# An attention unit's loads taken forward, transposes ahead of products, and a last row reordered, in a fused decoder block

## The chip, the cores and the metric

The kernel runs on one core of one Trainium2 chip. The metric is the device time of one execution in microseconds; lower is better. The version before takes 911.03 us, the median of 3 runs (910.79 to 912.06). The execution that was profiled took 911.87 us, and its span from the first to the last instruction is 910.2 us.

The core has four computing engines, each with its own queue of instructions that it takes strictly in order: TensorE (PE in the profile, its weight loads PEld), VectorE (DVE), ScalarE (ACT) and GpSimd (POOL). SyncE (SP) only issues transfers. Transfers issued by SP, POOL or ACT run on the same 16 DMA engines.

## The reference

One block of a decoder for 1024 tokens of width 1024, in float32:

```
h     = rmsnorm(x, norm_g) * (1 + scale) + shift      # scale, shift, gate from c @ w_ada
q, k, v, g_attn, xr, g_rnn, m_attn, m_rnn = split(h @ w_in)
q, k  = partial rotary embedding                       # 16 heads of 64, 4 of k and v
y_attn = window_attention(q, k, v, sinks) * silu(g_attn)     # window of 128 tokens
xr    = causal convolution of width 4
y_rnn = rg_lru(xr) * silu(g_rnn)                       # a scan along the tokens
merged = sigmoid(m_attn) * (y_attn @ w_attn_proj) + sigmoid(m_rnn) * (y_rnn @ w_rnn_proj)
x     = x + gate * (merged @ w_out)
out   = rmsnorm(x, final_g)
```

The attention works in blocks of 128 tokens: each block of queries sees its own block of keys and the one before, under a band mask, and a learned sink per head stands in the denominator.

## The kernel before

Every float32 operand of a large product is split into a rounded high part and the rest, and each product is made of three (high x high, high x low, low x high). Large products are tiled 128 x 128 against 512 columns and use one step of Strassen's scheme, so that a pair of output chunks takes seven slots of twelve matmuls each (`product`, line 709). Splitting the weights is the helper pair of lines 105 (ScalarE casts the high part, `wh`) and 111 (VectorE subtracts, `wl`).

The stages follow each other on TensorE: the start (to some 90 us), the seven-slot products of the projections with the gates of the recurrent branch between them (to some 557 us), attention in 32 units, between which the last projection slots and then the recurrent output projection (`rp`) are laid (to some 735 us), the projection of attention, and the output projection with the final norm in the tail (to the end). From the start to the end of attention the order on every engine is the order in which the program is written (a manual schedule); there is no scheduler in between. The functions that put work into slots keep estimated costs, but the change does not touch those.

The recurrent branch, per 128 channels: `conv(ic)` makes the convolved input `xc` on ScalarE (`base`, line 902) and VectorE (`tap`), in tiles that hold 4 KB per partition, two of them. Gate products follow, and `after_gates` computes the recurrence; its step `d2` (line 1053) multiplies by `xc` for the last time. In the last group of channels (c = KC - 1 = 7) that is the last use of any `xc` tile.

Attention. `open_attn` opens the memory pools of this stage and issues the first loads (two pairs of keys and queries, and the values). `load_kq(m)` loads the keys (`ks`) and queries (`qs`) of two units; there are two buffers. A unit u of the loop runs, on the engines named:

- `scores`: eight matmuls into `s_ps` (PE, line 1324); PSUM holds one `s_ps`, so the next scores need the last VectorE reading of this one
- `maxima_a`, `maxima_d`: copy to `p` (ACT, 1333), mask (DVE, 1339; in the first unit of a group POOL, 1342) and row maximum (DVE, 1344)
- `weights_a(u-1)`: four exponentials (ACT, 1349)
- pieces of the projections (one slot of twelve matmuls on PE, with their casts and subtractions)
- `weights_d(u-1)`: division by the denominator (DVE, 1355 and 1356)
- `values(u-3)`: up to four products with `v` into `pv` (PE, 1397), of `phc`, `plc` and their masked copies `phm`, `plm`
- `join_a`, `join_d` (u-3): two copies `ob` of 64 partitions (ACT, 1406 and 1407) and two adds into `yq` (DVE, 1417 and 1418)
- `transposed(u-2)`: four transposes of `p` into `pt` (PE, 1363)
- `split_a`, `split_d` (u-2): `phc` (ACT, 1368) and `plc` (DVE, 1374) from `pt`
- `masks(u-2)`: `phm` and `plm` (POOL, 1383)

`phc`, `plc`, `phm`, `plm`, `pt` and `pv` have one buffer each.

The tail. Each of eight rows of 128 tokens gets its output products, an add of the residual (`add_to`, DVE, line 1867), a sum of squares (`square`, ACT, 1871), a root (`root`, ACT, 1882), a reciprocal (DVE, 1886), a scaling of one half on DVE (1887) and of the other on ACT (1889), and one store. The second half of each row enters last. For rows 4 to 7 that is the left half (LEFT), and the right half has been multiplied by the final weight before. Row 7 is made in two parts of 256 columns, c1 and c2, and stored in two halves by SP and ACT. The tail too is in written order on PE, ACT and DVE.

## Time and profile before

| what | us |
|---|---|
| median of 3 runs | 911.03 |
| the profiled execution | 911.87 |
| its span | 910.2 |
| PE busy | 896.9 |
| DVE busy | 718.4 |
| ACT busy | 566.6 |
| POOL busy | 128.7 |

A row of a timeline reads: start and duration in us, engine, line of the kernel, operation, output <- inputs, shapes, how many were merged, and in brackets how long the engine had stood idle before it and what ended that. A row of the stretches reads: from and to, length, busy time and count for PE, PEld, DVE, ACT and POOL, then the clock that TensorE was granted (1.00 is full), the busy share of the DMA engines and their GB/s. A row of the chain of waits has start, duration and what ran. Ends of matmuls are modelled and overlap the next one's start, so the starts are what counts.

### The profile page before, as it was taken

The page shows a single profiled execution, that of the slowest core. Times are in us where ns is not written, and L with a number is a line of the kernel's source. Part 1 is how long each engine was busy: PE and PEld are TensorE (multiplying, and loading weights), DVE is VectorE, ACT ScalarE, POOL GpSimd, SP SyncE. Part 2 cuts the span into 40 slices and gives each one's busy share as a digit, 9 for nine tenths or more (in the row PEclk, how much of TensorE's full clock was granted, in tenths as well). Part 3 has the DMA queues.
Part 4 walks back from the last instruction along what each step waited for, and adds up shares of the span by engine and source line. Part 5 has one row for each costly group of instructions (what it writes and reads, how often), then busy time and mean ns, then how long its engine had stood idle before and what let it go on. Part 6 is the DMA issues. An engine that isn't in the chain of part 4 may idle for free.

```text
span 910.2 us, 12600 instructions
## 1 busy us (share of the span) xinstructions
PE 896.9 (99%) x4258; PEld 746.8 (82%) x4259; DVE 718.4 (79%) x1071; ACT 566.6 (62%) x1102; POOL 128.7 (14%) x216
## 2 busy tenths in 40 slices
PE   9999999999999999999999998999999999999996
PEld 6789888888888888888888887888888888888885
DVE  6997688988669875897797796899999847668855
ACT  7965554654566855777585874888888632115435
POOL 7420241200000000000000002353443400000000
PEclk9999999999999999999999999999999999999999
DMA  9828589862435353354535367996656289416604
GB/s 361 329 78 276 168 264 321 254 219 93 150 131 194 128 209 137 125 196 142 169 140 177 107 205 251 322 396 213 220 201 213 73 302 368 139 47 231 208 1 184
DMA packets 87203, 180.71 MB, mean 199 GB/s; under 512 B 8626, under 2 KB 29122, under 8 KB 87140
## 3 DMA queue, kind: packets, MB, share of 16 engines
q1 hardware_dynamic: 83056, 167.07, 52.3%
q0 software_dynamic: 3936, 12.59, 4.3%
q8 instruction: 33, 0.54, 0.2%
q14 instruction: 30, 0.25, 0.1%
q10 hardware_dynamic: 148, 0.27, 0.1%
HBM read 121.34 MB, written 58.95 MB: 198 GB/s over the span
## 4 chain that ended last, share of the span: by engine, by line
PE 91%; DVE 5%; ACT 2%; issue 1%; DMA 1%; POOL 0%; SPq 0%; DVEq 0%; ACTq 0%
PE bk L709 47%; PE rp L173 13%; PE out L1853 6%; PE pmain L173 5%; PE pgate L1022 5%; PE s_ps L1324 3%; PE pv L1397 2%; PE pmain L485 2%; PE bk L485 2%; PE pt L1363 1%; PE pmain L1574 1%; PE pmain L1573 1%; PE pmain L1572 1%; DMA qs<-q_d 1%; ACT jk L1871 1%
## 5 line engine op out<-in xcount | busy, mean ns | idle before, releaser
L709 PE MATMUL bk<-nl,wh 128*128 128x512 f32 x368 | 143.9, 391 | 0.0
L709 PE MATMUL bk<-nh,wh 128*128 128x512 f32 x368 | 143.8, 391 | 0.0
L709 PE MATMUL bk<-nh,wl 128*128 128x512 f32 x368 | 99.0, 391 | 0.0
L111 DVE TENSOR_TENSOR wl<-r,wh 128x512 fp32r<-128x512 f32 x109 | 79.2, 733 | 22.2 <-ACT wh L105 22.2
L105 ACT CAST wh<-r 128x512 fp32r<-128x512 f32 x107 | 65.5, 618 | 29.1 <-PE rp L173 9.8
L709 PEld LDWEIGHTS bk<-nh,wl 128*128 128x128 f32 x368 | 69.6, 189 | 14.6
L709 PEld LDWEIGHTS bk<-nh,wh 128*128 128x128 f32 x368 | 69.4, 189 | 14.5
L709 PEld LDWEIGHTS bk<-nl,wh 128*128 128x128 f32 x368 | 69.3, 188 | 14.3
L709 PE MATMUL bk<-hl,wh 128*128 128x512 f32 x184 | 71.6, 389 | 0.0
L709 PE MATMUL bk<-hh,wh 128*128 128x512 f32 x184 | 71.6, 389 | 0.0
L111 DVE TENSOR_TENSOR wl<-ws,wh 128x512 fp32r<-128x512 f32 x76 | 52.0, 685 | 7.1 <-ACT wh L105 7.0
L62 POOL DMA_DIRECT2D yh_d<-av x1 | 0.6, 569 | 371.6 <-ACT av L1085 371.6
L1349 ACT ACTIVATE p<-p,small 128x129 f32<-128x129 f32 x128 | 50.1, 401 | 0.0
L709 PE MATMUL bk<-hh,wl 128*128 128x512 f32 x184 | 49.2, 389 | 0.0
L105 ACT CAST wh<-ws 128x512 fp32r<-128x512 f32 x76 | 46.0, 614 | 4.7 <-DVE ws L731 2.3
L709 PEld LDWEIGHTS bk<-hh,wl 128*128 128x128 f32 x184 | 34.5, 188 | 7.2
L709 PEld LDWEIGHTS bk<-hh,wh 128*128 128x128 f32 x184 | 34.6, 188 | 7.1
L709 PEld LDWEIGHTS bk<-hl,wh 128*128 128x128 f32 x184 | 34.5, 188 | 7.1
L1324 PE MATMUL s_ps<-ks,qs 128*128 128x256 f32 (+1 forms) x256 | 37.6, 289 | 2.7 <-DMA qs<-q_d 2.5
L709 PE MATMUL bk<-hha,wh 128*128 128x512 f32 x92 | 35.8, 389 | 0.0
L709 PE MATMUL bk<-hla,wh 128*128 128x512 f32 x92 | 35.8, 389 | 0.0
L1324 PEld LDWEIGHTS s_ps<-ks,qs 128*128 128x128 f32 x256 | 32.4, 189 | 3.7 <-issue 2.8
(375 smaller groups left out, 2294.1 us busy)
## 6 DMA issues: line engine op xcount, KB each, us to landing
r<-w_main SPq DMA_DIRECT2D x100, 256.0 KB, 4.3
wada<-w_ss SPq DMA_DIRECT2D x16, 512.0 KB, 9.0
qs<-q_d SPq DMA_DIRECT2D x16, 512.0 KB, 5.1
wo_d<-wr SPq DMA_DIRECT2D x28, 256.0 KB, 2.9
wo<-wo_d SPq DMA_DIRECT2D x14, 512.0 KB, 5.3
ks<-k_d SPq DMA_DIRECT2D x12, 384.0 KB, 4.0
xt<-x SPq DMA_DIRECT2D x8, 512.0 KB, 6.6
sma_d<-c SPq DMA_DIRECT2D x16, 256.0 KB, 4.5
```

The source lines that it names most:

```text
L105: A.copy(dst[0][:], src)
L111: V.tensor_tensor(out=dst[1][:], in0=src, in1=f32(dst[0][:]), op=ALU.subtract)
L173: mm = T.matmul(ps[hf], ww, xx[kc][hf], start=(kc == 0 and ww is w_h and xx is xh), stop=(kc == KC - 1 and xx is xl))
L485: T.matmul(starts[c][hf], ww[:, c0:c0 + P], xh[kc][hf], start=(kc == 0 and t_ == "h"), stop=(kc == KC - 1 and t_ == "l"))
L709: W["pe"] = T.matmul(ps, ww[:, kc * P:(kc + 1) * P], b[kc][i], start=(first and n == 0), stop=(n == 11), skip_group_check=not first)
L1022: W["pe"] = T.matmul(ps[:, SL[hf]], ww[:, c0:c0 + P], xx_[:, SL[hf]], start=(ic == 0 and i == 0), stop=(ic == 1 and i == 2))
L1324: W["pe"] = T.matmul(o, qs[:, j, qc], ks[:, kb:n % 2 + 2, b, :], start=(b == 0), stop=(b == 1))
L1349: A.activation(px[:, j, :], px[:, j, :], AF.Exp, bias=sm[:, 0, j:j + 1], accum_out=sm[:, 1, j:j + 1])
L1363: W["pe"] = T.transpose(pt[:, j, :], px[:, j, 0:P], ident[:])
L1397: W["pe"] = T.matmul(pv[:], b, m[:].rearrange("p j q -> p (j q)"), start=(i == 0), stop=(i == len(prods) - 1))
L1572: T.matmul(o, hh[kc][th][:, ts_], wh[:, cols], start=(kc == 0), stop=False)
L1853: T.matmul(o, a[k][x_][:, p * P:(p + 1) * P], b[k][y_][:, cols], start=(first and k == 0 and i == 0), stop=(k == 3 and i == 2), skip_group ...
```

## The change

Three edits that do not depend on each other.

First, the tiles `xc` of the convolution get a pool of their own, at the other end of the memory (the right side, where the tiles of v's preparation stood before). As soon as the last multiplication by `xc` is written, that pool is closed, a pool for the keys and queries of even pairs of units takes its place, and the first load of keys and queries is issued there and then. `open_attn` opens only the pool for odd pairs and loads the second pair. Second, within a unit the transposes go ahead of the products with v, and the splits ahead of the joins. Third, the tail: row 7's squares are summed on DVE instead of ACT, and row 7's second add and square go ahead of the scaling of row 6's left half and of row 6's store; row 7's left half is scaled by root and weight in one instruction instead of two products with the weight and one with the root.

```diff
--- before.py
+++ after.py
@@ -872,8 +872,11 @@
 
     rn_ctx = ExitStack()
 
+    xc_ctx = ExitStack()
+
     def open_rnn():
         rope_ctx.close()
+        W["xcp"] = pool(xc_ctx, "xcp", bufs=2, side="right")
         W["rn"] = pool(rn_ctx, "rnn")
 
     def xr_sinks(hb):
@@ -898,7 +901,7 @@
                 x_ = xr[ic]
 
                 def base():
-                    t["xc"] = W["rn"].tile([P, S], F32, tag="xc", name="xc", bufs=2)
+                    t["xc"] = W["xcp"].tile([P, S], F32, tag="xc", name="xc")
                     A.activation(t["xc"][:], x_[:], AF.Identity,
                                  scale=pcol(PK_CW + 24, c), bias=pcol(PK_CB, c))
 
@@ -1052,6 +1055,10 @@
         def d2():
             V.tensor_tensor(out=t["it"][:], in0=t["it"][:], in1=W["xc", hb, oc][2][:],
                             op=ALU.mult)
+            if c == KC - 1:
+                xc_ctx.close()
+                W["kq", 0] = pool(at_ctx, "kq0", side="right")
+                load_kq(0)
 
         def a3():
             A.activation(tl("th"), t["rz"][:], AF.Tanh)
@@ -1276,23 +1283,22 @@
         nonlocal at, psx
         psm_ctx.close()
         psx = pool(psx_ctx, "psx", space=PSUM)
-        W["kq"] = pool(at_ctx, "kq", bufs=2, side="right")
+        W["kq", 1] = pool(at_ctx, "kq1", side="right")
         W["yo"] = pool(at_ctx, "yo", side="right")
         W["pp"] = pool(at_ctx, "pp", bufs=3, side="right")
         W["pp"].tile([P, 72], F32, name="pad", bufs=1)
         at = pool(at_ctx, "at", side="right")
-        load_kq(0)
+        load_kq(1)
         load_v(0)
-        load_kq(1)
 
     def load_kq(m):
         g, t0 = m // 4, (m % 4) * 256
-        ks = W["kq"].tile([P, 3, 2, P], F32R, tag="ks", name="ks")
+        ks = W["kq", m % 2].tile([P, 3, 2, P], F32R, tag="ks", name="ks")
         kv = k_d.rearrange("(p j) n b t -> j p n b t", j=4)[g]
         n0 = t0 // P
         lo = 1 if t0 == 0 else 0
         dma(ks[:, lo:, :, :], kv[:, n0 - 1 + lo:n0 + 2, :, :])
-        qs = W["kq"].tile([P, 4, 256], F32R, tag="qs", name="qs")
+        qs = W["kq", m % 2].tile([P, 4, 256], F32R, tag="qs", name="qs")
         dma(qs[:], q_d[g][m % 4].rearrange("(a j) t -> a j t", j=4))
         U["kq", m] = ks, qs
 
@@ -1701,14 +1707,16 @@
         flush()
         if 1 <= u < 33:
             weights_d(u - 1)
+        if 2 <= u < 34:
+            transposed(u - 2)
         if u >= 3:
             values(u - 3)
+        if 2 <= u < 34:
+            split_a(u - 2)
+            split_d(u - 2)
+        if u >= 3:
             join_a(u - 3)
             join_d(u - 3)
-        if 2 <= u < 34:
-            transposed(u - 2)
-            split_a(u - 2)
-            split_d(u - 2)
         if u + 1 < 32:
             sink(u + 1)
         while own_stores:
@@ -1941,23 +1949,32 @@
             result(4 + p, RIGHT, LEFT)
     c1, c2 = slice(0, 256), cut
     f = fs[:, 7, :]
+
+    def square_d(sl, acc):
+        jk = tail.tile([P, 2, HALF], F32, tag="S", name="xg", bufs=4)[:, 0, 0:256]
+        V.scalar_tensor_tensor(out=jk, in0=xo[7][:, sl], scalar=1.0, in1=xo[7][:, sl],
+                               op0=ALU.mult, op1=ALU.mult, accum_out=acc)
+
     gemm(pa[3][:, c1], A22, wt4, 3, cols=c1)
     add_to(7, c1, pa[3][:, c1])
-    square(7, c1, f[:, 1:2])
-    result(6, RIGHT, LEFT)
-    xg = tail.tile([P, 2, HALF], F32, tag="S", name="xg", bufs=4)[:, 0, :]
-    V.tensor_tensor(out=xg[:, c1], in0=xo[7][:, c1], in1=fg_bc[:, c1], op=ALU.mult)
+    square_d(c1, f[:, 1:2])
     V.scalar_tensor_tensor(out=f[:, 0:1], in0=f[:, 1:2], scalar=1.0 / D, in1=f[:, 0:1],
                            op0=ALU.mult, op1=ALU.add)
+    r6 = fs[:, 6, 3:4]
+    V.reciprocal(r6, fs[:, 6, 2:3])
+    A.activation(xo[6][:, RIGHT], xo[6][:, RIGHT], AF.Copy, scale=r6)
     gemm(end, A22, wt4, 3, cols=c2)
     add_to(7, c2, end)
-    square(7, c2, f[:, 1:2])
+    square_d(c2, f[:, 1:2])
+    V.scalar_tensor_tensor(out=xo[6][:, LEFT], in0=xo[6][:, LEFT], scalar=r6,
+                           in1=fg_bc[:, LEFT], op0=ALU.mult, op1=ALU.mult)
+    dma(out[6 * P:7 * P, :], xo[6][:])
     root(7)
-    V.tensor_tensor(out=xg[:, c2], in0=xo[7][:, c2], in1=fg_bc[:, c2], op=ALU.mult)
     V.reciprocal(f[:, 3:4], f[:, 2:3])
     A.activation(xo[7][:, RIGHT], xo[7][:, RIGHT], AF.Copy, scale=f[:, 3:4])
-    V.tensor_scalar(out=xg, in0=xg, scalar1=f[:, 3:4], scalar2=None, op0=ALU.mult)
-    dma(out[7 * P:, LEFT], xg)
+    V.scalar_tensor_tensor(out=xo[7][:, LEFT], in0=xo[7][:, LEFT], scalar=f[:, 3:4],
+                           in1=fg_bc[:, LEFT], op0=ALU.mult, op1=ALU.mult)
+    dma(out[7 * P:, LEFT], xo[7][:, LEFT])
     dma(out[7 * P:, RIGHT], xo[7][:, RIGHT], A)
     last.close()
 
```

SP's issues around the first edit, as one piece of the difference; `r` are weights of the projections, `gg` a gate, `wo_d` and `ga_d` stores of intermediate results:

```order
 L62 DMA gg<-sgr_d_135 128x1024
 L62 DMA r<-w_main 128x512
+L62 DMA ks<-k_d 128x512
+L62 DMA qs<-q_d_89 128x1024
 L62 DMA wo_d_140<-wr 128x512
 L62 DMA ga_d_94<-c 128x2x256
```

The same two loads stood behind two stores of `wo_d`, directly ahead of the second pair of ks and qs; now these fourteen rows of the old order, sixteen transfers, lie behind them, and the second pair follows after them.

TensorE in a unit of attention, before; then the same place with the change (its line numbers are 6 higher):

```order
L173 MATMUL rp_5727<-yl,wh 128x512 x2
L1397 MATMUL pv<-phc,vd 128x512
L1397 MATMUL pv<-plc,vd 128x512
L1397 MATMUL pv<-phm,vd 128x512
L1397 MATMUL pv<-plm,vd 128x512
L1363 MATMUL pt<-ident,p 128x128 x4
L1324 MATMUL s_ps<-ks,qs 128x256 x8
```

With the change:

```order
L173 MATMUL rp_5734<-yl,wh 128x512 x2
L1369 MATMUL pt<-ident,p 128x128 x4
L1403 MATMUL pv<-phc,vd 128x512
L1403 MATMUL pv<-plc,vd 128x512
L1403 MATMUL pv<-phm,vd 128x512
L1403 MATMUL pv<-plm,vd 128x512
L1330 MATMUL s_ps<-ks,qs 128x256 x8
```

The transposes moved past the four products; the scores stay last. On ScalarE and VectorE the split of the weights moved past the joins in the same way.

VectorE at the end, before; `xo` is a row, `rbig` holds the sums and roots, `xg` the weighted left half of row 7 (below: scratch for the squares):

```order
L1867 TENSOR_TENSOR xo<-xo,out_8241 128x256
L1886 RECIPROCAL rbig<-rbig 128x1
L1887 SCALAR_TENSOR_TENSOR xo<-xo,rbig,fg_bc 128x512
L1949 TENSOR_TENSOR xg<-xo,fg_bc 128x256
L1950 SCALAR_TENSOR_TENSOR rbig<-rbig 128x1
L1867 TENSOR_TENSOR xo<-xo,out_8242 128x256
L1956 TENSOR_TENSOR xg<-xo,fg_bc 128x256
L1957 RECIPROCAL rbig<-rbig 128x1
L1959 TENSOR_SCALAR xg<-xg,rbig 128x512
```

With the change:

```order
L1875 TENSOR_TENSOR xo<-xo,out_8249 128x256
L1955 SCALAR_TENSOR_TENSOR xg,rbig<-xo 128x256
L1961 SCALAR_TENSOR_TENSOR rbig<-rbig 128x1
L1964 RECIPROCAL rbig<-rbig 128x1
L1875 TENSOR_TENSOR xo<-xo,out_8250 128x256
L1955 SCALAR_TENSOR_TENSOR xg,rbig<-xo 128x256
L1969 SCALAR_TENSOR_TENSOR xo<-xo,rbig,fg_bc 128x512
L1973 RECIPROCAL rbig<-rbig 128x1
L1975 SCALAR_TENSOR_TENSOR xo<-xo,rbig,fg_bc 128x512
```

The scaling of row 6 (1887 before, 1969 now) stood ahead of row 7's second add and now stands behind it and its square.

## The prediction

> **What bounds the kernel now.** I read the page first, then the chain of waits in order of time, then the stretches on that chain that are not TensorE's, each by its timeline.
>
> ```profile
> PE 896.9 (99%) x4258; PEld 746.8 (82%) x4259; DVE 718.4 (79%) x1071; ACT 566.6 (62%) x1102; POOL 128.7 (14%) x216
> PE 91%; DVE 5%; ACT 2%; issue 1%; DMA 1%; POOL 0%; SPq 0%; DVEq 0%; ACTq 0%
> ```
>
> TensorE sets the time, so an edit pays only where TensorE stands still, runs slowly, or has finished. The chain leaves it in three places after the start-up: near 557, between 583 and 609, and from 884 on.
>
> First place, the entry to attention. The rows are the timelines of TensorE, VectorE and SP, a row of the chain, and three stretches with the granted clock behind the five busy times:
>
> ```profile
> 556.52 1.07 PE L709 MATMUL bk<-nh,wl 128*128 128x512 f32 x4
> 552.63 7.28 DMA qs<-q_d
> 560.04 1.08 PE L1324 MATMUL s_ps<-ks,qs 128*128 128x128 f32 x8 [2.45 <-DMA qs<-q_d]
> 557.43:560.04 2.61, 0.16 (x2) 0.03 (x1) 0.00 (x0) 0.00 (x0) 0.00 (x0) 1.00 1.02 385
> 560.04:565.36 5.32, 5.32 (x21) 4.36 (x22) 2.49 (x4) 1.59 (x3) 0.92 (x3) 0.68 0.99 358
> 565.36:569.05 3.69, 3.69 (x21) 3.21 (x20) 1.82 (x3) 2.54 (x11) 0.00 (x0) 1.00 0.65 207
> ...
> 522.39 0.42 SPq L62 DMA_DIRECT2D r<-w_main  x1
> 525.27 1.20 DVE L1053 TENSOR_TENSOR it<-it,xc 128x1024 f32<-128x1024 f32 x1
> 527.70 0.38 SPq L62 DMA_DIRECT2D ga_d<-c  x1
> 538.64 0.95 SPq L62 DMA_DIRECT2D r<-w_main  x2
> 545.75 5.33 SPq L62 DMA_DIRECT2D ga_d<-c  x2
> 554.96 0.36 SPq L62 DMA_DIRECT2D qs<-q_d  x1
> ```
>
> The first scores wait for qs, which takes 7.28 us because the DMA engines are full (share 1.02) and because its issue stood behind a store that held SP for 5.33 us. Matmuls of 512 columns start 0.23 us apart (two of them make the 0.46 between two kinds of unit, below), so after the four of 556.52 the scores could have started at 557.43. The wait costs 2.61 us. There is a second cost: after it the same work, eight score matmuls and twelve of 512 columns, takes 5.32 us at a clock of 0.68, and 3.69 at 1.00. The short form of unit 0 is worth some 0.03, so 5.32 - 3.66 = 1.66 us are lost to the clock.
>
> Second place, the units of attention. One starts with each s_ps:
>
> ```profile
> 587.78 1.19 PE L1324 MATMUL s_ps<-ks,qs 128*128 128x256 f32 x8
> 592.82 1.19 PE L1324 MATMUL s_ps<-ks,qs 128*128 128x256 f32 x8
> 597.48 0.51 PE L1397 MATMUL pv<-plm,vd 128*128 128x512 f32 x1
> 598.18 1.09 PE L1324 MATMUL s_ps<-ks,qs 128*128 128x128 f32 x8
> 603.16 1.19 PE L1324 MATMUL s_ps<-ks,qs 128*128 128x256 f32 x8
> 608.71 1.22 PE L1324 MATMUL s_ps<-ks,qs 128*128 128x256 f32 x8 [0.24 <-DVE p L1339]
> 614.06 1.19 PE L1324 MATMUL s_ps<-ks,qs 128*128 128x256 f32 x8
> 618.64 1.19 PE L1324 MATMUL s_ps<-ks,qs 128*128 128x256 f32 x8
> 623.88 1.22 PE L1324 MATMUL s_ps<-ks,qs 128*128 128x256 f32 x8
> ```
>
> A unit without a stall takes 592.82 - 587.78 = 5.04 us. The others show 5.36, 5.55, 5.35 and 5.24: 0.32 + 0.51 + 0.31 + 0.20 = 1.34 us lost in all. (The unit from 614.06 has two products with v less, hence 4.58.) Two of the stalls, 0.32 and 0.31, stand before the fourth product (plm, the mask that POOL makes last); two before the scores, which need VectorE's p. I count on nothing from the later units.
>
> Third place, the tail.
>
> ```profile
> 902.50 0.30 ACT L1882 ACTIVATE rbig<-rbig 128x1 f32<-128x1 f32 x1
> 903.03 0.75 DVE L1887 SCALAR_TENSOR_TENSOR xo<-xo,rbig,fg_bc 128x512 f32<-128x512 f32 x1
> 903.85 0.33 SPq L62 DMA_DIRECT2D out<-xo  x1
> 904.11 0.41 DVE L1867 TENSOR_TENSOR xo<-xo,out 128x256 f32<-128x256 f32 x1
> 904.61 0.42 ACT L1871 ACTIVATE jk<-xo 128x256 bf16<-128x256 f32 x1 [0.80 <-DVE xo L1867]
> 905.68 0.72 ACT L1958 ACTIVATE xo<-xo,rbig 128x512 f32<-128x512 f32 x1 [0.23 <-DVE rbig L1957]
> 906.20 0.33 SPq L62 DMA_DIRECT2D out<-xg  x1
> 906.43 0.38 ACTq L62 DMA_DIRECT2D out<-xo  x1
> 902.56 0.28 PE L1853 MATMUL out<-wo,ml 128*128 128x256 f32 x1
> GB/s 0 0 0 0 0 0 0 0 0 0 0 322 354 0 148 412 116 0 386 291 0 206 412 58 32 391 254 0 248 412 16 79 407 190 37 391 248 0 0 0
> ```
>
> TensorE ends at 902.84, but the last add waits until 904.11 behind row 6's scaling; the last issue is at 906.43 and the span ends at 910.2. The rates are in steps of 0.775 us from 880: row 6 moves from about 904.65 to 905.94 (0.80 us after its issue), row 7 from about 907.05 to 908.39, both at about 400 GB/s.
>
> **The change part by part.** *The early load.* ks and qs of unit 0 move from behind the store of 545.75 to behind the r of 522.39, and SP then waits for the product with xc, 525.27 + 1.20 = 526.47. Two issues of some 0.4 each (the rows of SP) end at about 527.3; with even the old 7.28 us they land by 535, 22 us before use. Behind them on SP stand a store of wo_d, the ga_d of 527.70 and two stores of y. None is loaded soon, and the next loads that weights need are those of 538.64, which today wait for another store. I cost the move at nothing; SP would have to be held some 11 us more before those loads suffer. The convolution tiles change their place, and the first one now waits for stores of v's parts instead of stores of q, which are older: nothing. Next late in the same place would be the second pair of loads, issued by 554.96; with even 9 us they are there at 564, and unit 2 would need them at 569.05 - 4.27 = 564.78. That is the thinnest cover, and 0.79 MB less in front of it makes it thicker. So 2.61 us go. With no gap I expect the clock to stay at 1.00, and 1.66 more go: **-4.27**. From below: only the wait, -2.6; from above -4.4.
>
> [...] The row speaks for the gap, as 0.68 stands right behind it.
>
> *The order within a unit.* No instruction is added or removed. The four transposes (5.04 less 3.69 for scores and twelve products, less 0.91, so 0.44 us) pass ahead of the four products with v (4 x 0.23 = 0.91), and the splits ahead of the joins on ScalarE and VectorE. So pt ends 0.91 us earlier, phc no longer waits for two copies on ScalarE, plc no longer stands behind two joins on VectorE, and the products are wanted 0.44 later. VectorE falls behind here for two reasons, the first row and the fourth:
>
> ```profile
> 589.06 0.42 DVE L1417 TENSOR_TENSOR yq<-pv,ob 64x256 f32<-64x256 f32 x1 [0.61 <-ACT ob L1407]
> 596.25 0.68 DVE L1532 TENSOR_TENSOR yq<-yq,r 128x512 f32<-128x512 f32 x1
> 600.79 1.11 POOL L1383 TENSOR_SCALAR_AFFINE_SELECT plm<-plc 128x512 fp32r<-128x512 f32 x1 [0.65 <-DVE plc L1374]
> 601.32 1.12 DVE L1532 TENSOR_TENSOR yq<-yq,r 128x512 f32<-128x512 f32 x1
> ...
> 594.74 0.59 ACT L1368 CAST phc<-pt 128x512 fp32r<-128x512 f32 x1
> ```
>
> It waits 0.61 us for the copies (a wait that remains, since plc now waits for phc instead), and the same instruction takes 1.12 beside POOL's mask and 0.68 alone. After the change the two joins stand right behind plc, so they run beside that mask, and they read PSUM. Standing behind plc, the joins let plm start 2 x 0.42 us sooner, which covers the stalls of 0.32 and 0.31; each overlap that falls away gives VectorE 0.44 back before the scores at 608.71 and 623.88. The most is 1.34. The least is nothing: if VectorE keeps its pace, TensorE only arrives earlier and waits for p instead (rival A). A loss would need a longer loop through the single phc buffer (rival E). I take **-1.2**, near the upper end, as plm's lead is the larger effect.
>
> [...]
>
> *The tail.* Two squares leave ScalarE for VectorE, two products with the final weight vanish into one scaling, and row 6's scaling of the left half and its store pass behind row 7's last add. Nearest rows for the square with its sum:
>
> ```profile
> 18.60 1.26 DVE L275 SCALAR_TENSOR_TENSOR jk<-wada,c_bc 128x1024 bf16<-128x1024 f32 x1
> 19.79 0.08 DVE L275 DVE_READ_ACCUMULATOR jk<-wada,c_bc 128x1 f32 x1
> ```
>
> For 256 columns it lies between an add of that width (0.41) and a scaling of 512 (0.75); by the slope 0.75 to 1.26 I take 0.49, and 0.08 for the sum. The first square falls into VectorE's wait for the root of row 6, which ends at 902.80. The reciprocal ends near 903.0, as now; the add follows at once (now at 904.11), the square from 903.43 to 904.0, row 6's scaling to 904.75: its store is issued at 904.77, 0.92 later than now. The root of row 7 runs beside that; its reciprocal ends near 904.91, the last scalings near 905.66, and the last issue is at 905.68 against 906.43, 0.75 earlier. But now two rows follow each other: row 6 would start at 904.77 + 0.80 = 905.57, and 2 x 0.524 MB at 400 GB/s take 2.62, so 908.19 against 908.39. **-0.2**; -0.75 if the transfers pack better, +0.3 if the square with its sum costs 0.3 more each and row 6 goes out later still.
>
> Sum: -4.27 - 1.2 - 0.2 = -5.7. The profiled execution took 911.87 us around a span of 910.2; the span becomes 904.5 and that time 906.2. The median of the runs shown, 911.03, lies 0.84 below the profiled one; I take the difference from it: **905.3 us**.
>
> **The rivals.**
>
> A. VectorE keeps setting the pace of attention. For: its wait of 0.61 stays in another place, and it was late by itself at 608.71. Against: the 0.44 of each overlap that goes is its own time. Only the entry and the tail pay: 911.03 - 4.47 = 906.6.
>
> B. The slow clock stays although the gap has gone: -2.61 - 1.2 - 0.2, so 907.0. Against it: 1.00 both before and after the one slow stretch.
>
> C. The DMA engines become the wait. The rows show shares of 1.02 and 0.99, and TensorE now comes 4.3 us sooner to operands of y that pass through the same engines. For relief there are 0.79 MB less (128 x 1536 words; 2.0 us at 400 GB/s) and the free third of 565 to 569 (0.35 x 3.69 = 1.3 us): 4.27 - 2.0 - 1.3 = 1.0 us could be given back, 906.3; with unit 2's keys late as well, up to 907.4. Against: today no product waits for a transfer but the first.
>
> D. The early load does not end the wait, because something else holds the first scores. Then -1.4, 909.6, which is no change. Against: all other needs of that instruction are met long before.
>
> E. Slower. phc has one buffer. Its next writer must now wait for a product that stands behind the transposes, so a loop closes: transposes 0.44, product 0.23, phc 0.59, plc at most 0.75 (a scaling of that width), plm 1.11, with some 0.4 for hand-overs 3.5 us. It decides when it passes the period of 5.04. If ScalarE's other work put 1.8 us into it, each further 0.25 over 29 units would cost 7.2: 911.03 - 4.5 + 7.2 = 913.7. Against: 1.5 us of room.
>
> **How the numbers follow.** Forecast 0.57 (its own range 904.3 to 906.2), A 0.14, B 0.07, C 0.10, D 0.05, E 0.04, and 0.03 for more than the forecast (all three upper ends give -4.4 - 1.34 - 0.75, 904.5, and stalls that I did not count). A measurement of this kernel tells 0.2% (1.8 us) from no change, so A, B and C count as faster: 0.91, same 0.05, slower 0.04. The range for 8 in 10 leaves out D, E and the ends: 904.2 to 907.5.
>
> **What would show it.** Right: TensorE without a gap at 557, a clock of 1.00 from 557 to 566, and 3.66 us from the first scores to the second; periods of 5.04 up to 624; the last issue some 0.8 us nearer to TensorE's end, with DMA rates at 400 GB/s unbroken over the last two rows. Wrong: a gap at 557 with another releaser (D); a slow clock with no gap (B); s_ps that waits for p with periods above 5.2 (A); a product that waits for yh, yl or ks (C); periods above 5.04 in all units with phc as releaser (E). The prediction fails as a whole if TensorE's end in the tail does not move by over 4 us.

## The result

The changed kernel takes 907.68 us, the median of 6 runs (907.29 to 908.05), beside 911.45 for the kernel before (6 runs, 909.81 to 912.79). The ratio is 0.9959 with a 95% interval of 0.9946 to 0.9972: 0.4% faster. A second comparison on another chip gave 907.62 beside 911.75 and a ratio of 0.9953 (0.9936 to 0.9970). The direction was forecast; 905.3 was too low by 2.4 us, and 907.68 lies just outside the range. The profiled execution took 907.33 us, with a span of 905.5.

The page of the changed kernel, in the order of the two rows that the prediction began with, and one group:

```profile
PE 894.3 (99%) x4259; PEld 746.1 (82%) x4259; DVE 718.6 (79%) x1073; ACT 567.2 (63%) x1098; POOL 121.1 (13%) x216
PE 93%; DVE 4%; ACT 2%; issue 1%; DVEq 0%; ACTq 0%
L111 DVE TENSOR_TENSOR wl<-r,wh 128x512 fp32r<-128x512 f32 x109 | 75.0, 695 | 24.0 <-ACT wh L105 23.7
```

The transfer of qs has left the chain of waits, and TensorE's share of it rose from 91% to 93%. POOL's busy time fell from 128.7 to 121.1 us without an instruction less: the 28 masks plm take 632 ns in the mean, against 979 before.

The first place, the entry to attention, in the timeline of TensorE and as three stretches (from and to, length, busy time of the five engines, granted clock, share of the DMA engines, GB/s):

```profile
556.85 1.07 PE L709 MATMUL bk<-nh,wl 128*128 128x512 f32 x4
557.75 1.00 PE L1330 MATMUL s_ps<-ks,qs 128*128 128x128 f32 x8
552.00:557.75 5.75, 5.75 (x27) 4.74 (x26) 4.56 (x7) 1.62 (x3) 3.35 (x4) 1.00 1.00 304
557.75:561.43 3.68, 3.68 (x22) 3.15 (x21) 0.00 (x0) 1.59 (x3) 0.64 (x1) 1.00 0.98 367
561.43:565.13 3.70, 3.70 (x22) 3.21 (x21) 3.38 (x6) 2.55 (x11) 0.31 (x2) 1.00 0.71 264
```

The scores start 0.90 us after the start of the last group of four matmuls, without a gap. The clock is 1.00 throughout, and unit 0 takes 3.68 us, although the DMA engines are still full (0.98).

The second place, the units. Rows of TensorE, then of VectorE and POOL in the same stretch:

```profile
599.15 1.11 PE L1330 MATMUL s_ps<-ks,qs 128*128 128x256 f32 x8
605.00 1.22 PE L1330 MATMUL s_ps<-ks,qs 128*128 128x256 f32 x8 [0.63 <-DVE p L1345]
597.27 1.10 DVE L1548 TENSOR_TENSOR al<-yq,ah 128x512 fp32r<-128x512 f32 x1
...
600.30 1.06 DVE L1362 TENSOR_TENSOR p<-p,small 128x512 f32<-128x512 f32 x1
...
602.42 0.43 DVE L1424 TENSOR_TENSOR yq<-pv,ob 64x256 f32<-64x256 f32 x1
...
604.21 0.73 DVE L1345 COPY_PREDICATED p<-mgt,s_ps 128x512 f32<-128x512 uint32 x1
597.20 0.63 POOL L1348 TENSOR_SCALAR_AFFINE_SELECT p<-p 128x512 f32<-128x512 f32 x1
600.18 0.64 POOL L1389 TENSOR_SCALAR_AFFINE_SELECT phm<-phc 128x512 fp32r<-128x512 f32 x1 [1.16 <-ACT phc L1374]
602.21 0.63 POOL L1389 TENSOR_SCALAR_AFFINE_SELECT plm<-plc 128x512 fp32r<-128x512 f32 x1 [1.40 <-DVE plc L1380]
```

Unit 10's scores (605.00) still wait for VectorE's p, and longer than before: the unit ahead of them takes 5.85 us against 5.55. VectorE has no idle time in this stretch. Two of its instructions run beside a mask of POOL and take 1.10 and 1.06 instead of some 0.69, 0.78 us in all; the unit takes 0.79 more than 5.06.

The third place, the tail, with the rates in steps of 0.75 us from 876:

```profile
898.59 0.40 DVE L1875 TENSOR_TENSOR xo<-xo,out 128x256 f32<-128x256 f32 x1
899.37 0.75 DVE L1969 SCALAR_TENSOR_TENSOR xo<-xo,rbig,fg_bc 128x512 f32<-128x512 f32 x1
900.98 0.40 ACTq L62 DMA_DIRECT2D out<-xo  x1
GB/s 0 0 0 11 0 0 0 0 0 0 0 344 355 0 126 404 169 0 322 377 0 82 426 191 0 273 393 27 66 399 262 0 0 268 404 363 361 3 0 0
```

TensorE ends at 898.51 now, and the last add starts 0.08 us later instead of 1.27. The last issue stands 2.47 us behind TensorE's end instead of 3.59, but the two last rows now move as one block (268 to 404 GB/s), and the span ends 7.02 us behind it instead of 7.32.

Put together from these rows, by stretches of the program, with a second pair of executions beside it (a second profile of each kernel, from the experiments):

| stretch | forecast | first pair | second pair |
|---|---|---|---|
| start to the last matmul ahead of attention | 0 | +0.33 | +0.27 |
| from there to the scores of unit 1 | -4.27 | -4.26 | -4.33 |
| scores of unit 1 to scores of unit 31 | -1.2 | +0.21 | +0.80 |
| from there to the first output product | 0 | -0.55 | -0.53 |
| output products | 0 | -0.05 | -0.03 |
| TensorE's end to the end of the span | -0.2 | -0.30 | -0.30 |
| span | -5.7 | -4.63 | -4.11 |

### The profile page after: what moved, and what is told of

Read it like the earlier page. It is cut to its first block, busy times and chain, and to the rows that moved or that the text cites. A ratio compares the mean times of both kernels' runs of the same rounds, so it can differ in the third digit from the quotient of the medians.

```text
span 905.5 us, 12663 instructions
## 1 busy us (share of the span) xinstructions
PE 894.3 (99%) x4259; PEld 746.1 (82%) x4259; DVE 718.6 (79%) x1073; ACT 567.2 (63%) x1098; POOL 121.1 (13%) x216
## 4 chain that ended last, share of the span: by engine, by line
PE 93%; DVE 4%; ACT 2%; issue 1%; DVEq 0%; ACTq 0%
PE bk L709 48%; PE rp L173 13%; PE out L1861 6%; PE pmain L173 5%; PE pgate L1025 5%; PE s_ps L1330 3%; PE pv L1403 3%; PE pmain L485 2%; PE bk L485 2%; PE pt L1369 1%; PE pmain L1580 1%; PE pmain L1579 1%; PE pmain L1578 1%; ACT jk L1879 1%; DVE xo L1875 1%
## 5 line engine op out<-in xcount | busy, mean ns | idle before, releaser
L111 DVE TENSOR_TENSOR wl<-r,wh 128x512 fp32r<-128x512 f32 x109 | 75.0, 695 | 24.0 <-ACT wh L105 23.7
L1330 PEld LDWEIGHTS s_ps<-ks,qs 128*128 128x128 f32 x256 | 34.4, 189 | 3.7 <-DVE p L1345 1.1
L1330 PE MATMUL s_ps<-ks,qs 128*128 128x256 f32 (+1 forms) x256 | 35.3, 280 | 0.6 <-DVE p L1345 0.6
```

Of the source, the lines that this page charges most:

```text
L111: V.tensor_tensor(out=dst[1][:], in0=src, in1=f32(dst[0][:]), op=ALU.subtract)
L1330: W["pe"] = T.matmul(o, qs[:, j, qc], ks[:, kb:n % 2 + 2, b, :], start=(b == 0), stop=(b == 1))
```

## The experiments

**Each part taken back.** Theory: the load gives some 4.2 us and the tail 0.3, and the order within a unit nothing, since VectorE sets the pace in units 7 to 10. Rival: the order is worth its 1.2, and the earlier start of attention took that away.

The old order in the changed kernel:

```diff
-        if 2 <= u < 34:
-            transposed(u - 2)
         if u >= 3:
             values(u - 3)
+            join_a(u - 3)
+            join_d(u - 3)
         if 2 <= u < 34:
+            transposed(u - 2)
             split_a(u - 2)
             split_d(u - 2)
-        if u >= 3:
-            join_a(u - 3)
-            join_d(u - 3)
```

> The changed kernel with the order within a unit as it was before (products with v, joins, transposes, split). Early load and new tail stay. From the first scores to the first scores of unit 31 the changed kernel took 709.96 - 557.75 = 152.21 us, the one before 148.35 from unit 1 on against 148.53 now. If the new order is worth its 1.2 us as forecast and the earlier start of attention ate it, this stretch gets 1.2 us longer here and the time 908.9. If the new order is worth next to nothing, because VectorE's work sets the pace in units 7 to 10 in any order, the stretch stays within 0.3 us and the time is 907.4 to 908.0.

Measured: 908.11 us (907.08 to 908.87), ratio to the kernel before 0.9971 (0.9960 to 0.9983). Against the changed kernel's 907.62 to 907.68, on other chips, this tells no difference beyond what such a comparison can tell. The profile is clearer. Its scores:

```profile
594.49 1.09 PE L1330 MATMUL s_ps<-ks,qs 128*128 128x128 f32 x8
599.48 1.19 PE L1330 MATMUL s_ps<-ks,qs 128*128 128x256 f32 x8
604.94 1.22 PE L1330 MATMUL s_ps<-ks,qs 128*128 128x256 f32 x8 [0.18 <-DVE p L1345]
```

From unit 0 to unit 31 it takes 151.43 us, 0.78 less than the new order, with stalls of 0.32 (unit 8) and 0.42 (unit 10). From there to the first output product it takes 112.61, 0.53 more. So the new order costs 0.78 in the loop and gives 0.53 back in the drain. Neither theory had it so: the order is worth nothing that the times can tell, by two terms of opposite sign.

The late load in the changed kernel:

```diff
                 W["kq", 0] = pool(at_ctx, "kq0", side="right")
-                load_kq(0)
...
-        load_kq(1)
+        load_kq(0)
         load_v(0)
+        load_kq(1)
```

> The changed kernel with the first keys and queries loaded where they were before; pools, order within a unit and tail are the new ones. If the early load is what removed the gap and the slow clock, both are back: a wait for qs of 2.3 to 2.9 us at 557, a granted clock of 0.68 in the 5.3 us behind it, and the time is 4.3 above the changed kernel's, 912.0, with a scatter between runs of over 1 us, since the wait hangs on DMA engines that are full. If the slow clock had another cause than the gap, the time is about 910.3 or the clock is slow somewhere without a gap. If the wait was removed by something else in the change, the time stays near 907.7.

Measured: 910.84 us (909.00 to 913.68), ratio 1.0002 (0.9990 to 1.0014). So the early load carries the whole gain, as far as these intervals can tell: 1.0002 less 0.9959 is 0.43%, 3.9 us (4.5 by the second comparison). The gap was there, but shorter, and the slow clock was not:

```profile
560.42 1.08 PE L1330 MATMUL s_ps<-ks,qs 128*128 128x128 f32 x8 [1.44 <-DMA qs<-q_d]
558.90:560.42 1.52, 0.08 (x2) 0.04 (x1) 0.00 (x0) 0.00 (x0) 0.00 (x0) 1.00 1.01 394
560.42:564.15 3.73, 3.73 (x20) 3.22 (x21) 1.22 (x3) 1.59 (x3) 0.91 (x3) 1.00 1.01 362
```

This execution lost 1.7 us at the entry (1.61 until the scores, 0.06 in unit 0), not 4.27; the rest of what its span has more than the changed kernel's (3.23 in all) lies in the start (1.06) and in units 1 to 31 (0.49). What the load is worth differs from execution to execution. The spread that was expected is there: 4.7 us, against some 0.8 in either comparison of the changed kernel.

The old tail in the changed kernel (from row 7's first add on, the lines of the kernel before):

```diff
-    square_d(c1, f[:, 1:2])
+    square(7, c1, f[:, 1:2])
+    result(6, RIGHT, LEFT)
...
-    dma(out[7 * P:, LEFT], xo[7][:, LEFT])
+    dma(out[7 * P:, LEFT], xg)
```

> The changed kernel with the tail as before. From the end of TensorE's last matmul to the end of the span the kernel before took 7.32 us, the changed one 7.02. My step (two rows of 0.524 MB back to back at 400 GB/s bind, although the last issue is earlier) expects 7.3 again and a time 0.2 to 0.4 above the changed kernel's, 908.0. If the earlier last issue (by 1.1 us against TensorE's end) were what counts, it is 908.8. If nothing of the tail's gain is real, 907.7.

Measured: 908.58 us (907.89 to 909.00), ratio 0.9976 (0.9966 to 0.9986). TensorE's end to the span's end is 7.31 us, against 7.02 to 7.04 in every execution with the new tail. So the part is worth 0.3 us, although the last issue comes 1.1 us sooner.

The splits ahead of the joins, but the products ahead of the transposes as before:

```diff
-        if 2 <= u < 34:
-            transposed(u - 2)
         if u >= 3:
             values(u - 3)
         if 2 <= u < 34:
+            transposed(u - 2)
             split_a(u - 2)
             split_d(u - 2)
```

> The changed kernel with the products with v ahead of the transposes again, but the splits still ahead of the joins on ScalarE and VectorE. It takes the two halves of the reordering apart. If the steady units' 0.02 us (5.06 against 5.04) comes from TensorE's new order and the masks' lead from the split's place, the steady units are back at 5.04 and the time is 0.3 to 0.5 below the changed kernel's, 907.3. If the lead comes from the earlier transposes, pt is 0.91 us later here, VectorE waits for phc with the joins behind it, and the units get longer: 908.0 to 910.

Measured: 908.49 us (907.76 to 909.49), ratio 0.9973 (0.9963 to 0.9983). In its profile the steady units take 5.04 us again, so the 0.02 belongs to TensorE's order. But the scores of units 7, 8, 10, 12, 13 and 21 come 5.21, 5.29, 5.28, 4.85 (for 4.59), 5.43 and 5.56 us after the ones ahead, and units 1 to 31 take 149.38 us, against 148.53 with both halves and 147.75 with neither. The split's place alone makes it worse: pt is as late as before, and VectorE now waits for phc (0.40 and 0.43 us in two of these units) with the joins behind it.

The rows of a steady unit show where the 0.02 comes from, the new order first (629.96 and on), then the old one (633.99 and on, kernel before):

```profile
629.96 1.11 PE L1330 MATMUL s_ps<-ks,qs 128*128 128x256 f32 x8
630.91 0.63 PE L173 MATMUL rp<-yh,wh 128*128 128x512 f32 x2
...
634.02 0.47 PE L1403 MATMUL pv<-phc,vd 128*128 128x512 f32 x1
634.33 0.39 PE L1403 MATMUL pv<-plc,vd 128*128 128x512 f32 x1
```

```profile
633.99 1.19 PE L1324 MATMUL s_ps<-ks,qs 128*128 128x256 f32 x8
635.02 0.63 PE L173 MATMUL rp<-yh,wh 128*128 128x512 f32 x2
...
637.77 0.39 PE L1397 MATMUL pv<-phc,vd 128*128 128x512 f32 x1
637.99 0.39 PE L1397 MATMUL pv<-plc,vd 128*128 128x512 f32 x1
```

In these rows whatever follows the four transposes pays. The first product with v takes 0.31 us to the next start instead of 0.22, while the scores, now behind a product of 512 columns, take 0.95 instead of 1.03. The two nearly cancel in the loop. In the drain there are no scores, and something pays in either order: with the old one a pair of projection matmuls (0.55 instead of 0.46), with the new one the product still. So most of the 0.53 that the drain gains is something else, a stall of the old order before the product with plm, here in the kernel before:

```profile
722.03 0.39 PE L1397 MATMUL pv<-phm,vd 128*128 128x512 f32 x1
722.54 0.51 PE L1397 MATMUL pv<-plm,vd 128*128 128x512 f32 x1
```

From start to start this takes 0.51 us instead of 0.23. In units_old it takes 0.54, with POOL's plm as releaser; the new order has no such row.

**Does VectorE's sum hold up unit 10?** The gating of y is a product (0.68 us) and, a unit later, a subtraction (0.69) on VectorE, and while attention catches up two units in a row begin one. This kernel begins it in odd units only; no work is left out.

```diff
-            if late and ("gq", late[0]) in U and u >= loaded[late[0]] + 2:
+            if u % 2 and late and ("gq", late[0]) in U and u >= loaded[late[0]] + 2:
```

> The changed kernel with the gating of y (the product of 0.68 us, the rounded copy and the subtraction of 0.69 us on VectorE and ScalarE) begun only in odd units, so that no unit has two starts behind each other while attention catches up; one condition is added, no work is taken away. If VectorE's sum of work over units 7 to 10 is what makes unit 10's scores wait (5.85 us from unit 9 to unit 10 and 5.18 to unit 11, against 5.06), these become 5.1 or less and the time falls by 0.7 to 1.0 us to about 906.8. If the wait came from the new order itself (phc behind the transposes, joins last), it stays at 0.6 us or more and the time at 907.7.

Measured: 907.22 us (906.58 to 907.68), ratio 0.9953 (0.9939 to 0.9968). Its scores:

```profile
599.96 1.11 PE L1330 MATMUL s_ps<-ks,qs 128*128 128x256 f32 x8
605.02 1.10 PE L1330 MATMUL s_ps<-ks,qs 128*128 128x256 f32 x8
610.08 1.10 PE L1330 MATMUL s_ps<-ks,qs 128*128 128x256 f32 x8
```

The stall is gone (5.06 and 5.06), so the wait came from VectorE's sum and not from the loop through phc. Between the medians, on different chips, lie 0.4 to 0.5 us and not 0.7 to 1.0, and the ratio to the kernel before is that of the changed kernel's second comparison, so these times alone don't show a gain. In the profiled execution units 1 and 2 took 0.29 us more, at a place that the edit does not touch. VectorE's first maximum waits there for a store of the recurrent branch (562.65 here, 561.65 in the changed kernel), which stands in DMA engines that are still full (share 0.99 from 558.00 to 561.65 in the changed kernel).

**What makes the clock slow?** In the kernel before the granted clock is 0.50 for 3.413 us from 561.72 on, and again from 906.46 to the end; the two starts lie 101 times 3.413 us apart. A piece is from here on a stretch of 3.413 us counted from such a change, and a slow piece one at half the clock. These kernels put a gap of chosen length ahead of the first scores.

```diff
+        if u == 0:
+            z = at.tile([P, 4, P], F32R, tag="phc", name="z")
+            T.matmul(s_ps[:, 0, 0:P], ident[:], ident[:], start=True, stop=True)
+            V.tensor_copy(z[:, 0, :], s_ps[:, 0, 0:P])
+            for i in range(5):
+                V.tensor_copy(z[:, (i + 1) % 4, :], f32(z[:, i % 4, :]))
+            T.matmul(s_ps[:, 0, 0:P], z[:, 1, :], z[:, 1, :], start=True, stop=True)
```

> The changed kernel with an artificial gap on TensorE ahead of the first scores: a small product, six copies of 128x128 on VectorE one after the other, and a small product that reads the last one. The results of both products are overwritten. The gap should be some 1.5 us. Theory of a gap that must be long (the gap of 2.6 us before slowed the clock, the one of 1.5 us with the late load did not): no slow clock here, the first scores 1.7 us later than in the changed kernel and everything behind them too. Theory of a fixed grid (the granted clock changes in pieces of 3.41 us, and a piece in which TensorE idles for about half of it, more than 1.0 and at most 1.7 us, is followed by a slow one): slow or not by where the gap falls on the grid; with 1.5 us in one piece it may be slow, split over two it is not.

> The same with nine copies, a gap of some 2.2 us. Gap theory: threshold between 1.5 and 2.6, so either. Grid theory: slow if 1.7 us or more of it fall in one piece of the grid, not slow if no piece holds more than 1.0 us. A slow piece costs 3.41 x 0.5 = 1.7 us.

> The same with twelve copies, a gap of some 2.9 us. Gap theory: longer than the 2.6 us of the kernel before, so always a slow piece of 3.41 us behind it. Grid theory: at least 1.45 us of it lie in one piece, and slow if 1.7 us or more do.

Measured: gaps of 1.69, 2.47 and 3.26 us; one execution each, 909.96, 912.61 and 912.52 us. The first was followed by no slow piece (clock 1.00 over the 3.84 us behind it), the other two by one each (0.69 over 5.45 and over 5.48 us). Stretches of such pieces, of the kernel before, then of the first and the second of these:

```profile
558.30:561.72 3.42, 1.68 (x12) 1.57 (x13) 0.00 (x0) 0.56 (x2) 0.00 (x0) 1.00 1.00 350
561.72:565.13 3.41, 3.41 (x10) 2.63 (x9) 2.49 (x4) 1.03 (x3) 0.92 (x3) 0.50 1.03 395
```

```profile
559.39:562.81 3.42, 2.48 (x15) 2.24 (x16) 0.78 (x4) 1.17 (x3) 0.51 (x1) 1.00 1.00 380
562.81:566.22 3.41, 3.41 (x20) 3.00 (x19) 2.77 (x5) 1.32 (x5) 0.44 (x3) 1.00 0.66 248
```

```profile
559.79:563.20 3.41, 1.85 (x13) 1.72 (x14) 1.33 (x6) 0.54 (x2) 0.00 (x0) 1.00 1.04 403
563.20:566.61 3.41, 3.41 (x10) 2.63 (x9) 2.49 (x4) 1.06 (x3) 0.91 (x3) 0.50 0.29 112
```

The pieces in which TensorE works 1.68 and 1.85 of 3.41 us (0.49, 0.54) are followed by one at 0.50; the one with 2.48 (0.72) is followed by one at 1.00. Both readings, length and grid, fit these. So two kernels have such a gap ahead of the scores of every unit from 8 on, with four and seven copies of 64 columns.

> The changed kernel with a gap ahead of the scores of every unit from 8 on: a small product, four copies of 128x64 on VectorE one after the other, a small product that reads the last. The results of both products are overwritten. Each gap should be 1.1 to 1.6 us, or somewhat more where VectorE is behind. If the length of a gap decides, no piece of the clock is slow, since 1.69 us was not followed by one. If the share of a piece of 3.41 us that TensorE works decides (0.49 and 0.54 were followed by a slow piece, 0.70 and more were not), slow pieces come only behind pieces in which it worked less than 0.54 to 0.70, and with 1.4 us (0.59) the single gap is at the edge, so few or none.

> The same with seven copies, gaps of 1.6 to 2.2 us. If the length decides, all gaps of about one length act alike. If the grid decides, gaps of one length act differently: those that lie within one piece (work in it 0.36 to 0.53) are followed by a slow one, those split over two pieces (0.68 and more in each) are not.

Measured: 1051.28 and 1073.80 us. The gaps came out at 3.3 to 5.7 and 3.9 to 6.4 us, much longer than meant, since the copies wait behind VectorE's other work. So the test of equal gaps of some 1.5 us was not made. But the clock is slow for a part of the two: its mean is 0.95 and 0.94, against 0.995 in the kernel before beside them. Three pieces of the first kernel, with one gap of 3.26 us over two of them, and two further ones:

```profile
695.42:698.83 3.41, 2.04 (x12) 1.61 (x11) 1.34 (x3) 1.99 (x4) 1.52 (x4) 1.00 0.00 0
698.83:702.25 3.42, 1.52 (x11) 1.49 (x12) 1.69 (x6) 0.55 (x2) 0.97 (x2) 1.00 0.23 60
702.25:705.66 3.41, 3.41 (x9) 2.68 (x9) 2.30 (x4) 1.92 (x9) 0.00 (x0) 0.50 0.75 195
593.02:596.44 3.42, 1.53 (x11) 1.22 (x8) 3.25 (x6) 3.07 (x9) 0.82 (x2) 1.00 1.01 402
596.44:599.85 3.41, 0.00 (x0) 0.00 (x0) 3.27 (x9) 0.00 (x0) 0.63 (x1) 1.00 1.02 405
```

The share of work alone doesn't tell the pieces apart. Those with 0.45 (698.83), 0.49 and 0.54 were followed by a slow one; the 0.45 of 593.02 was not. Another measure does tell these apart: the length of an idle stretch of TensorE, counted from the stretch's own start, also where that lies in the piece ahead, to its end or to the end of the piece, whichever comes first. It is 2.45 us in the kernel before (piece of 558.30), 2.47 in gap_8 (559.79) and 3.26 in many_3 (698.83), and each of these pieces was followed by a slow one. It is 1.44 us in load_late, 1.69 in gap_5, and in many_3 1.37 at 698.83, where the gap of 3.26 enters the next piece, and 1.88 at 596.44; there the clock stayed at 1.00. So both readings hold in part in these rows: the length of the gap tells the pieces apart, but only as far as the gap has come by the end of a piece. This was read off the profiles afterwards; no run was made to test it, and these rows show nothing between 1.88 and 2.45 us. At the start of the program it does not seem to hold: in load_late six matmuls of 512 columns start 0.41 to 0.43 us apart from 25.45 to 27.56, as in the slow piece of the kernel before (0.42 to 0.43 in its second profile), where the changed kernel has 0.22 to 0.24, and no idle stretch from 15 us to there is above 0.68 us. That stays open.

**The kernel before, once more**

> The kernel before once more, one look. If the spread of its times (909.2 to 912.6) comes from the wait for qs and from whether a slow piece of the clock follows it, a fast execution shows a gap below 2 us at 557 and no slow piece, and one above 911.5 shows a gap of 2.5 us or more with one. If the spread comes from elsewhere, the gap and the slow piece are there at any time.

Measured: 911.65 us, with a gap and a slow piece, as expected of a time above 911.5:

```profile
560.47 1.59 PE L1324 MATMUL s_ps<-ks,qs 128*128 128x128 f32 x8 [2.52 <-DMA qs<-q_d]
560.47:565.79 5.32, 5.32 (x20) 4.55 (x21) 2.37 (x4) 1.59 (x3) 0.91 (x3) 0.68 0.96 360
598.61 1.09 PE L1324 MATMUL s_ps<-ks,qs 128*128 128x128 f32 x8
...
609.05 1.21 PE L1324 MATMUL s_ps<-ks,qs 128*128 128x256 f32 x8 [0.18 <-DVE p L1339]
614.11 1.19 PE L1324 MATMUL s_ps<-ks,qs 128*128 128x256 f32 x8
```

The stalls are not the ones that the prediction counted: 0.32, 0.43, 0.02 and nothing, 0.77 us in all, where the first profile had 1.34. A faster execution of this kernel was not caught in a profile; that its gap is shorter and without a slow piece is shown for the late load alone.

**A faster version.** Two kernels were run beside the changed one on one chip, which took 907.62 us there (907.22 to 908.02).

> The changed kernel itself, as the measure for the two kernels beside it: 907.3 to 908.1, no gap at the first scores, unit 10's scores 0.6 us late for VectorE's p.

The first has the paced gating and stores row 6 in two halves:

```diff
     A.activation(xo[6][:, RIGHT], xo[6][:, RIGHT], AF.Copy, scale=r6)
+    dma(out[6 * P:7 * P, RIGHT], xo[6][:, RIGHT])
...
-    dma(out[6 * P:7 * P, :], xo[6][:])
+    dma(out[6 * P:7 * P, LEFT], xo[6][:, LEFT])
```

> The paced kernel, and row 6 stored in two halves: the right half as soon as ScalarE has scaled it, the left half where the whole row is stored in the changed kernel. If the last two rows are bound by the rate of their transfers, as my step on the tail says, 0.26 MB move some 0.7 us sooner and the span ends 0.4 to 0.7 us nearer to TensorE's end (7.02 now): time 906.6. If the end hangs on the last issue and what follows it alone, nothing changes: 7.0, and 907.2 as for the paced kernel.

Measured: 906.26 us (906.00 to 907.24), ratio to the kernel before 0.9940 (0.9925 to 0.9955). The span ends 6.49 us behind TensorE's end instead of 7.02. The rates in the same steps as above:

```profile
GB/s 0 11 0 0 0 0 0 0 0 93 415 191 0 289 404 6 71 404 224 0 251 410 38 33 393 257 11 224 399 104 8 361 331 355 344 0 0 0 0 11
```

The last block still runs at 331 to 361 GB/s without a break, but it starts sooner, so the rate of the transfers was the bound, as the prediction had it.

The second also returns to the old order in the loop and keeps the new one for the drain (u of 32 and more):

```diff
+        if u < 32:
+            if u >= 3:
+                values(u - 3)
+                join_a(u - 3)
+                join_d(u - 3)
+            if 2 <= u:
+                transposed(u - 2)
+                split_a(u - 2)
+                split_d(u - 2)
+        else:
...
```

> The same kernel with the order within a unit as before the change (products, joins, transposes, split) for all units up to 31 and the new order only for the three passes that drain the loop. If the new order costs 0.02 us in each steady unit and pays only in the drain (112.08 against 112.61 us from unit 31's scores to the first output product), and pacing takes the stalls of either order away, this is 0.4 to 0.5 us below paced_halves: 906.2. If the old order keeps its own stalls (0.32 and 0.42 us in units 8 and 10 without pacing), it is 0.2 to 0.4 above it: 906.9.

Measured: 905.76 us (905.13 to 906.44), ratio 0.9933 (0.9918 to 0.9948), 1.9 us below the changed kernel beside it, with no run of the one inside the range of the other. Units 1 to 31 take 146.98 us, against 147.71 in paced_halves and 148.52 in the changed kernel, and no unit has a stall: with the gating paced, the old order needs no help. What is late next shows in its chain of waits (start, duration, what):

```profile
827.76 7.25 DMA wo<-wo_d
...
839.72 0.49 ACT out L1914
...
840.25 1.89 PE out L1869 x7
```

In this kernel TensorE reaches the output projection sooner than one of the transfers of its weights. ScalarE waits for that, its copies come late, and TensorE stands for 0.62 us at 840.25.

## Why the prediction was wrong, step by step

**The early load: right.** -4.27 was forecast and -4.26 and -4.33 came in the two pairs of profiles. No gap, clock 1.00, 3.68 us for unit 0. The moved issues cost nothing. Rivals B and D are out, and so is C as a wait of TensorE: the shares of 1.00 and 0.98 in the rows above held no matmul up (it may stand behind the 0.29 us of paced, by way of VectorE). What it did not see is that -4.27 is the price of one execution. With the late load a gap of 1.44 us without a slow piece cost 1.7. The gaps of 2.45 and 2.52 us in the two profiles of the kernel before were each followed by the slow clock, 0.68 over the next 5.32 us; with 1.44 us it stayed at 1.00.

**The order within a unit: wrong, and the step that fell.** "I take -1.2, near the upper end, as plm's lead is the larger effect." The two pairs give -0.34 and +0.27 for the loop and the drain together. One part of it held and two failed.

- What failed first: the upper end of 1.34 was read from one execution. The second profile of the kernel before has 0.77 us of these stalls, and so has the changed kernel with the old order.
- What held: plm's lead does cover the stall before the fourth product: the unit that took 5.36 takes 5.04 (589.07 to 594.11), and in the drain another such stall, of 0.28, is gone that the prediction did not count.
- What failed next: "Each overlap that falls away gives VectorE 0.44 back": POOL's sum fell, and so did the mean of the split of weights on VectorE (733 to 695 ns), but in the units that VectorE holds up the overlap only moved, from the split of weights to al (1.10) and the scaling of p (1.06). That is rival A, in one unit and with a price of 0.8, and the paced kernel shows it: take the load off VectorE there, and the stall is gone. The joins ran at 0.41 and 0.43 beside plm (602.00 and 602.42), as in the mean of all 32 units (412 and 428 ns); the step's mistake was to look at the joins alone.

Added to this are 0.02 us in each steady unit, 0.6 over the loop, for what follows the transposes. "No instruction is added or removed" was taken to mean that TensorE's own time stays. Rival E's sign (all units above 5.04) was there, but with no wait behind it; phc was never the releaser.

**The tail: right.** -0.2 forecast, -0.30 measured; 0.75 was expected of the last issue and 1.12 came, and the rate of two rows back to back ate the rest. The square with its sum took 0.42 us, near the 0.49 taken.

**From the profile to the median: wrong.** The prediction subtracted 0.84 us because the profiled execution before lay that much above its median. Half of that distance was the sample: the median of three runs was 911.03, that of six is 911.45. The rest may belong to the entry, as the profile had the long gap and the slow piece, which not every execution needs to have; this is not shown, and the second profile of the kernel before, with both, lies 0.10 below the median of the nine runs beside it. The new profile lies 0.35 below its own median. Of the 2.4 us, this step makes 1.2 (0.84 + 0.35) and the order within a unit 0.9; 0.3 is the start of the program, and the tail and the output products gave 0.15 back. The start scatters: in the profiles of the changed kernel and of the experiments on it, the last matmuls ahead of attention start anywhere from 556.63 to 558.05 us.

**The chances.** A was given 0.14, and its mechanism is what happened in the loop; its 906.6 was made with the same 0.84. A range built on one profile and three runs that spread over 1.3 us should have reached beyond 907.5.

## What to carry over

A stall that hangs on a transfer through full DMA engines has no one price (here 4.27 us in one execution and 1.7 in another): read it from two executions before it becomes a term, and do not carry the distance between profile and median over to a kernel in which that stall is gone. When an engine works at its limit over a few units, reordering can move its collisions only, as it did here (1.10 and 1.06 us for two instructions of some 0.69); spreading the work over more units took the stall away (5.06 us for 5.85). A reordering that pays in the drain of a loop (0.53 us here) can cost in its body (0.78), so choose the order for each apart.

## What was not expected of the hardware

In the kernel before, an idle stretch of TensorE of 2.45 us, shorter than one piece of 3.413, was followed by a piece at half the clock (0.50 from 561.72 to 565.13), which cost 1.66 us; behind 1.44 us (load_late) and 1.69 (gap_5) the clock stayed at 1.00. Where the stretch fell on the pieces did not save it: the 2.47 us of gap_8 lay with 0.91 in one piece and 1.56 in the next, TensorE still worked 0.54 of that piece, and the one behind it was at 0.50.

In the rows here the first instruction behind the four transposes of 128 columns took 0.08 to 0.09 us more to the next start than behind a matmul of 512 columns: 1.03 against 0.95 for the scores, 0.31 against 0.22 for the product with phc, 0.55 against 0.46 for a pair of projection matmuls.
